# A hybrid decoder layer on one Trainium2 core: attention's steps no longer fall within an output pair's last call of matmuls

## The chip, the core and the metric

The kernel runs on one core of a Trainium2 chip. Five engines matter here: TensorE (PE in the profile), VectorE (DVE), ScalarE (ACT), GpSimd (POOL) and the queue that issues most DMAs (SP). Each engine works through its own instructions in the order in which the program was built, and waits for the others by semaphores. The metric is the device time of one execution in microseconds; the median of three runs of the kernel before is 2708.38 us, the lowest 2703.49 and the highest 2708.49.

## What is computed

One layer of a decoder trunk, for 512 tokens of width 2048, in float32. Cut to what matters:

```python
h    = rmsnorm(x, attn_norm_g)
proj = h @ w_in                       # 2048 -> u, v_sgu, q, k, v_att (1024 each), g_a, g_b (2048 each)
y_a  = u * (tril(w_s) @ rmsnorm(gelu(v_sgu)) + b_s)          # per chunk of 128 tokens
# stick-breaking attention, 8 heads of 128, per block of 128 queries:
z        = q @ k.T * Dh ** -0.5
log_1m   = where(strict, log_sigmoid(-z), 0)
tail     = cumsum(log_1m, reverse=True) - log_1m
w        = where(strict, exp(log_sigmoid(z) + tail), 0)
y_b      = w @ v
merged = sigmoid(g_a) * (y_a @ w_up_a) + sigmoid(g_b) * (y_b @ w_up_b)
x = x + merged @ w_o
x = x + swiglu(rmsnorm(x))            # hidden width 5632
x = x + sigmoid(rmsnorm(x) @ w_ple_gate) * (p @ w_ple)
```

The change concerns the projection by `w_in` and the attention that runs beside it. Everything behind that stage is the same in both kernels.

## The kernel before, in words

**Pairs and calls.** A `Pair` makes 256 columns of a projection for all 512 tokens. In the stage of `w_in` it works by Strassen's seven products (`PRODUCTS`), with a high and a low part of each operand. The sum over the 2048 rows is cut into four calls of `Pair.add`, each with the weights of two blocks of rows. A call has 32 matmuls: products 0 to 4 have four each at L629, each into one of five whole PSUM banks ("ps"), and the last two have six each at L271 to L273, into the halves of a sixth bank. In the pair's **last call** (`stop`, L615), `mix_doubled` (L675 on) adds the finished products on DVE (L688) with copies by ACT (L685) while the call's other products are still being made.

**The order of work in the first stage.** `order` lists what the pairs make: q, k, v of round 0 (two heads each), then four gate blocks, then q, k, v of round 1 and three gates, round 2 and three gates, round 3 and four gates; then the eight blocks of the spatial gating and the last two gates. So a round has six or seven pairs, and its attention runs beside the pairs that follow its k.

**Ticks.** Within each call, `tick()` is called after the fourth product (i = 3) and after the seventh (i = 6) (`TICKS`, L643). A pair has four calls and so eight ticks; the seventh and eighth lie within its last call. A tick takes from the heap `waiting` whatever is due and lets it emit its next instructions. `beside(steps, first)` (L249) puts a generator there: `step` runs it to its next `yield n` and puts itself back n ticks later. What a tick emits is tied to stand behind the matmuls already emitted (`add_manual_dep`, L214); a scheduler then decides how far behind them.

**Attention.** A round's attention (L1013 on) is such a generator. It starts six ticks behind its k and makes one step a tick. For each of 8 blocks (two heads, j from 3 down to 0, (4 - j)*128 query columns) there are stages with these lines:

- stage a: z on PE into a small bank ("small", of which there are two) (L1034), scaled and through Abs, Exp, Ln on ACT (L1036 to L1039)
- stage m: two sums on DVE (L1043, L1045), a mask on POOL (L1047), and a copy and a memset of row 0 on POOL (L1054, L1055)
- stage b: the high part on ACT (L1058); stage c: the low part on DVE (L1062)
- stage d: two matmuls with a triangle of ones on PE (L1068 with the high part, L1069 with the low part, called tri 1 and tri 2 below), a subtraction on DVE (L1073, for j > 0 also L1071), the exponential on ACT (L1074), a mask on POOL (L1075)
- `finish(h)` after the four blocks of a head: the product with v on PE (L1084), a copy on ACT (L1086). Its first matmul reads block j = 0, the last one that was made.

A block i (0 to 7) has its steps b, c, d at ticks 9 + 3i, 10 + 3i and 11 + 3i behind k; `finish(0)` stands with step c of block 4 at tick 22, `finish(1)` at tick 34. q, k and v have their own preparation (`q_prep`, `k_prep`, `v_prep`): transposes on PE (L959), squares on ACT (L966), a power on POOL (L976) and scalings on ACT (L981).

**Weights.** Each call's weights come through one of the landing buffers. SP issues two DMAs for them (L316 and L318, "wholes<-w_in"). When they have landed, POOL issues a third one that adds to what landed (L338, in `landed`). Then ACT rounds them to a high part (L334), DVE makes sums (L350) and low parts (L331), and the buffer is free for SP's next load once DVE has read it. POOL's DMA issues stand in one queue with its masks.

Of the kernel before, what the change touches and what calls it, by code (L numbers as in the profile page):

```python
# [65 lines left out]
def hybrid_layer(  # L66
# [93 lines left out]
    def fits(sizes):  # L160

        before = parts.holes, wholes.holes
        parts.holes, wholes.holes = list(parts.holes), list(wholes.holes)
        try:
            for arena, n, how in sizes + [(wholes, 1024, "low")]:
                arena.take(n, how)
            return True
        except ValueError:
            return False
        finally:  # L170
            parts.holes, wholes.holes = before

    def wide():
        return tmp.tile([P, 1024], F32, tag="out", name=nm("out"))
# [7 lines left out]


    clock = [0]
    waiting = []
    newest = {}
    builds = deque()

    def mark(instruction):
        newest[instruction.ins.engine] = instruction.ins.name  # L190

    def after(n, fn):
        heapq.heappush(waiting, (clock[0] + n, next(names), fn))

    def traced():
        return nc.cur_bb.bb.instructions

    def tick():

        clock[0] += 1  # L200
        last, units = traced()[-1], dict(newest)
        for f in list(builds)[:AHEAD]:
            if not f.there and f.ready() and fits([(wholes, 1024, "old"), (wholes, 1024, "low")]):
                f.fetch()
                break
        if builds and builds[0].ready() and builds[0].arrived() and fits(builds[0].sizes):
            builds.popleft().step()
        while waiting and waiting[0][0] <= clock[0]:
            heapq.heappop(waiting)[2]()
        for i in reversed(traced()):  # L210
            if i is last:
                break
            if i.engine in units:
                tc.add_manual_dep(  # L214
                    i, units[i.engine],
                    mybir.DependencyInfo(mybir.DependencyClass.NoSync,
                                         mybir.DependencyReason.DATA),
                    reason="in its place among the units")
# [27 lines left out]
                self.advance()  # L246
            return self.result

    def beside(steps, first=1):  # L249


        def step():
            n = next(steps, None)
            if n is not None:
                after(n, step)

        after(first, step)
# [11 lines left out]
    def mm3(ps, sh, sl, mh, ml, start, stop, halved=False):  # L269
        for s in (slice(0, 256), slice(256, T)) if halved else (slice(None),):  # L270
            nc.tensor.matmul(ps[:, s], sh, mh[:, s], start=start, stop=False)  # L271
        nc.tensor.matmul(ps, sh, ml, start=False, stop=False)  # L272
        return nc.tensor.matmul(ps, sl, mh, start=False, stop=stop)  # L273
# [109 lines left out]
    def prepare_early():  # L383

        if prepared:
            prepared[0].to(4)
        if len(prepared) > 1 and (slots or prepared[1].step > 1):
            prepared[1].to(3)

    def prepare_late():  # L390

        if len(prepared) > 1 and prepared[1].step > 1:
            prepared[1].to(4)
        for w in list(prepared)[2:]:
            w.to(1)
        ahead(8)
# [175 lines left out]
    class Pair:  # L572
# [21 lines left out]
        def add(self, kind, ws, xs, prepare=True):  # L594
            n = len(ws)
            start = self.left[kind] == self.n[kind]
            self.left[kind] -= n
            stop = self.left[kind] == 0
            if prepare:
                prepare_early()  # L600
            if kind == "P":
                for u, ((wh, wl), (xh, xl)) in enumerate(zip(ws, xs)):
                    for ps, bs in zip(self.ends(), ((2, 3), (0, 1))):
                        for k, b in enumerate(bs):
                            first = start and u + k == 0

                            mark(mm3(ps, wh[:, b], wl[:, b], xh[k], xl[k],
                                     first and not self.both, stop and u == n - 1 and k == 1,
                                     first and self.both and b < 2))
                    if prepare and u == 0:  # L610
                        prepare_late()
                    tick()
                return

            if stop:  # L615
                o = self.home()
                self.o = wide() if o is None else o
                mix = (self.mix_doubled if self.doubled else self.mix)(self.o)
            for i, ((name, h), (w, x)) in enumerate(zip(HALVES, PRODUCTS)):
                for u, ((wh, wl), t) in enumerate(zip(ws, xs)):  # L620
                    first, last = start and u == 0, stop and u == n - 1
                    if i < self.doubled:
                        ps = self.at(i)
                        both = ps, wh[:, w], t[:, x].rearrange("p s c -> p (s c)")
                        low = ps[:, :256], wl[:, w], t[:, x, 0]

                        work = (low, both) if u else (both, low)
                        for k, (out, l, r) in enumerate(work):
                            m = nc.tensor.matmul(out, l, r, start=first and k == 0,  # L629
                                                 stop=last and k == 1)  # L630
                        mark(m)
                    else:


                        ps = self.at(name)[:, 256 * h : 256 * h + 256]
                        ends = not (self.both and name in "yz") and (h == 1 or name == "z")
                        mark(mm3(ps, wh[:, w], wl[:, w], t[:, x, 0], t[:, x, 1],
                                 first and h == 0, last and ends))
                if stop:
                    next(mix)  # L640
                if i == 2:
                    prepare_late()
                if i in TICKS[n]:  # L643
                    tick()

        def mix(self, o):

# [205 lines left out]
    def rms_tile():  # L853
        return tmp.tile([P, 8], F32, tag="rr", name=nm("rr"), bufs=4)
# [87 lines left out]
    def a_tiles():  # L942

        for tag, n in (("l", T), ("w0", T), ("w1", 3 * P), ("w2", 2 * P), ("w3", 2 * P),
                       ("first", 5 * P), ("k", 1024), ("v", 1024), ("zs", 1024)):
            att[tag] = take(n)
        for tag in ("zh", "zl"):
            att[tag] = parts.take(T, "high")

    def a_tile(tag, n=T, start=0):  # L950
        return att[tag].f(start, start + n)
# [50 lines left out]
    def k_prep(o, rk):  # L1002
        for h in range(2):
            yield 2
            token_rms(flip(o[:, h * T : (h + 1) * T]), rk[:, NT * h : NT * (h + 1)])
        nc.scalar.activation(o, o, AF.Copy, scale=gcol[:, g_k : g_k + 1])
# [156 lines left out]
    def block(w, i):  # L1163

        if w == "k":
            return a_tile("k", 1024)
        if w == "s":
            y_a[i] = take(1024)
            return y_a[i].f()
# [56 lines left out]
    for n, ((w, i), pr) in enumerate(zip(order, made())):  # L1226
        if n == 0:
            row1 = norm1.row()
            nc.vector.tensor_scalar(out=eps_cols, in0=norm1.mean, scalar1=EPS, scalar2=None,
                                    op0=ALU.mult)  # L1230
        if n == 0:
            a_tiles()
        o = pr.out(block(w, i) if n < 3 else None)
        if w == "q":
            beside(q_prep(o, i))
        elif w == "k":
            kT, rk = o, rms_tile()
            beside(k_prep(kT, rk))
            beside(attention(i, kT, rk, a_tile("v", 1024)), 6)
        elif w == "v":  # L1240
            beside(v_prep(o, a_tile("v", 1024)))
        elif w == "s":
            scaled(o, row1)
            nc.scalar.activation(o, o, AF.Gelu_apprx_tanh)
            beside(sgu_v(i, o))
        elif w == "u":
            scaled(o, row1)
            nc.scalar.activation(o, o, AF.Gelu_apprx_tanh)
            nc.vector.tensor_tensor(out=y_a[i].f(), in0=o, in1=y_a[i].f(), op=ALU.mult)
            y_done["a", i] = True  # L1250
        else:
            d = tc.dram_tile([P, 1024], F32, name=nm("gsp"))
            nc.sync.dma_start(out=d, in_=o)
            gate_spill[w, i] = d
# [92 lines left out]
    for c, kinds in enumerate(PASSES):  # L1347
        units, first = hs[at : at + len(kinds)], at
# [139 lines left out]
```

## Time and profile before

| what | value |
|---|---|
| median of three runs | 2708.38 us |
| the three runs | 2708.38, 2708.49, 2703.49 us |
| span of the profiled execution, first to last instruction | 2701.9 us |
| PE busy | 2668.1 us, 99% of the span |
| DVE busy | 2147.0 us, 79% |
| ACT busy | 1367.3 us, 51% |
| POOL busy | 459.0 us, 17% |
| mean TensorE clock granted | 0.997 of full |

The profiled execution's span is 6.5 us under the median of the runs; its time from outside is not among the numbers shown. The stage with the attention lies between about 87 us and 640 us of the span. "Busy" on PE is modelled: a matmul's row is longer than the distance to the next one, since they are pipelined, so a stall is somewhat longer than the idle time that the profile gives. "[0.88 <-DVE parts L1062]" at the end of a row of the timeline is the idle time of the engine before it, and what ended it.

### The profile page before, as it was taken

The page shows a single profiled execution, that of the slowest core. Times are in us where ns is not written, and L with a number is a line of the kernel's source. Part 1 is how long each engine was busy: PE and PEld are TensorE (multiplying, and loading weights), DVE is VectorE, ACT ScalarE, POOL GpSimd, SP SyncE. Part 2 cuts the span into 40 slices and gives each one's busy share as a digit, 9 for nine tenths or more (in the row PEclk, how much of TensorE's full clock was granted, in tenths as well). Part 3 has the DMA queues.
Part 4 walks back from the last instruction along what each step waited for, and adds up shares of the span by engine and source line. Part 5 has one row for each costly group of instructions (what it writes and reads, how often), then busy time and mean ns, then how long its engine had stood idle before and what let it go on. Part 6 is the DMA issues. An engine that isn't in the chain of part 4 may idle for free.

```text
span 2701.9 us, 43167 instructions
## 1 busy us (share of the span) xinstructions
PE 2668.1 (99%) x15875; PEld 2354.6 (87%) x15875; DVE 2147.0 (79%) x3621; ACT 1367.3 (51%) x2143; POOL 459.0 (17%) x543
## 2 busy tenths in 40 slices
PE   8999999999999999999999999999999999999999
PEld 6888888989998889988888888888888999988898
DVE  7687878787887566688988888888889667688776
ACT  7656565655554343374444444444445344453543
POOL 0232323232220000001111111111111111110110
PEclk9999999999999999999999999999999999999999
DMA  7677777777776467678888888888887668688784
GB/s 224 156 185 175 181 173 186 170 187 197 177 186 197 140 173 200 173 219 211 212 212 202 200 203 205 201 198 210 195 210 206 181 167 262 184 249 236 218 243 133
DMA packets 303268, 529.40 MB, mean 196 GB/s; under 512 B 25680, under 2 KB 162896, under 8 KB 303056
## 3 DMA queue, kind: packets, MB, share of 16 engines
q1 hardware_dynamic: 242304, 426.22, 49.9%
q0 software_dynamic: 60752, 100.43, 23.8%
q8 instruction: 124, 2.03, 0.3%
q14 instruction: 88, 0.72, 0.1%
HBM read 479.36 MB, written 47.19 MB: 195 GB/s over the span
## 4 chain that ended last, share of the span: by engine, by line
PE 88%; DVE 5%; DMA 2%; ACT 2%; issue 1%; POOL 1%; SPq 0%; DVEq 0%; ACTq 0%; POOLq 0%
PE ps L629 39%; PE ps L272 14%; PE ps L273 14%; PE ps L271 14%; PE small L629 4%; DVE wlo L331 2%; DVE out L688 1%; PE small L1084 1%; PE small L959 1%; ACT whi L334 1%; DMA wholes<-w_in 0%; DMA wholes<-w_first 0%; DVE wholes L350 0%; PE small L1034 0%; DVE parts L267 0%
## 5 line engine op out<-in xcount | busy, mean ns | idle before, releaser
L334 ACT ACTIVATE whi<-wholes 128x512 fp32r<-128x512 f32 (+4 forms) x950 | 857.6, 917 | 838.3 <-DVE wholes L350 261.9
L629 PE MATMUL ps<-parts,whi 128*128 128x512 f32 x3384 | 1134.8, 398 | 0.3 <-DVE p L688 0.3
L331 DVE TENSOR_TENSOR wlo<-wholes,whi 128x512 fp32r<-128x512 f32 (+4 forms) x950 | 962.4, 1046 | 101.0 <-ACT whi L334 100.5
L271 PE MATMUL ps<-parts,whi 128*128 128x256 f32 (+1 forms) x2675 | 855.1, 323 | 15.7 <-ACT parts L266 9.7
L272 PE MATMUL ps<-parts,whi 128*128 128x256 f32 (+1 forms) x2640 | 857.0, 325 | 1.0 <-DVE parts L267 0.8
L273 PE MATMUL ps<-parts,wlo 128*128 128x256 f32 (+1 forms) x2640 | 855.9, 325 | 0.9 <-DVE wlo L331 0.9
L629 PEld LDWEIGHTS ps<-parts,wlo 128*128 128x128 f32 x3384 | 635.8, 188 | 142.6 <-issue 1.0
L629 PE MATMUL ps<-parts,wlo 128*128 128x256 f32 x3384 | 671.1, 279 | 0.0
L271 PEld LDWEIGHTS ps<-parts,whi 128*128 128x128 f32 x2675 | 508.8, 190 | 60.7 <-ACT parts L266 10.8
L629 PEld LDWEIGHTS ps<-parts,whi 128*128 128x128 f32 x3384 | 545.3, 189 | 5.0 <-issue 1.0
L272 PEld LDWEIGHTS ps<-parts,whi 128*128 128x128 f32 x2640 | 502.7, 191 | 47.2 <-DVE parts L267 2.8
L273 PEld LDWEIGHTS ps<-parts,wlo 128*128 128x128 f32 x2640 | 502.7, 191 | 41.2 <-DVE wlo L331 2.8
L350 DVE TENSOR_TENSOR wholes<-wholes 128x256 f32<-128x256 f32 (+1 forms) x794 | 326.8, 412 | 21.8 <-DMA wholes<-w_ffn_out 4.0
L338 POOL DMA_DIRECT2D wholes<-w_ffn_in x172 | 149.7, 871 | 693.0 <-DVE wholes L350 238.8
L688 DVE TENSOR_TENSOR out<-out,ps 128x256 f32<-128x256 f32 x388 | 160.3, 415 | 131.7 <-ACT out L685 131.5
L338 POOL DMA_DIRECT2D wholes<-w_in x132 | 118.0, 895 | 486.1 <-DVE wholes L350 145.7
L655 DVE TENSOR_TENSOR out<-out 128x256 f32<-128x256 f32 x144 | 60.9, 423 | 114.7 <-ACT out L652 112.2
L629 PE MATMUL small<-parts,whi 128*128 128x512 f32 x344 | 136.5, 397 | 0.0
L267 DVE TENSOR_TENSOR parts<-wholes,parts 128x1024 fp32r<-128x1024 f32 (+4 forms) x131 | 123.7, 950 | 14.9 <-ACT parts L266 14.5
L266 ACT ACTIVATE parts<-wholes 128x1024 fp32r<-128x1024 f32 (+4 forms) x131 | 105.8, 834 | 42.0 <-DVE wholes L497 20.0
L338 POOL DMA_DIRECT2D wholes<-w_ffn_out x56 | 56.9, 1020 | 403.4 <-DMA wholes<-w_ffn_out 139.6
L1328 ACT ACTIVATE out<-out 128x512 f32<-128x512 f32 x44 | 27.8, 633 | 157.9 <-DVE out L1327 157.9
(121 smaller groups left out, 1655.0 us busy)
## 6 DMA issues: line engine op xcount, KB each, us to landing
wholes<-w_ffn_in SPq DMA_DIRECT2D x172, 384.0 KB, 5.6
wholes<-w_in SPq DMA_DIRECT2D x132, 384.0 KB, 4.9
wholes<-w_ffn_in SPq DMA_DIRECT2D x172, 256.0 KB, 4.8
wholes<-w_ffn_in POOLq DMA_DIRECT2D x172, 256.0 KB, 5.4
wholes<-w_in SPq DMA_DIRECT2D x132, 256.0 KB, 4.2
wholes<-w_in POOLq DMA_DIRECT2D x132, 256.0 KB, 5.0
wholes<-x SPq DMA_DIRECT2D x33, 512.0 KB, 5.5
wholes<-w_ffn_out SPq DMA_DIRECT2D x31, 512.0 KB, 4.5
```

Source lines behind the costliest of these rows:

```text
L266: return (nc.scalar.activation(hi, src, AF.Copy), nc.vector.tensor_tensor(out=lo, in0=src, in1=hi.bitcast(F32), op=ALU.subtract))
L267: nc.vector.tensor_tensor(out=lo, in0=src, in1=hi.bitcast(F32), op=ALU.subtract))
L271: nc.tensor.matmul(ps[:, s], sh, mh[:, s], start=start, stop=False)
L272: nc.tensor.matmul(ps, sh, ml, start=False, stop=False)
L273: return nc.tensor.matmul(ps, sl, mh, start=False, stop=stop)
L331: in_turn(nc.vector.tensor_tensor(out=self.lo[:, blocks], in0=r, in1=h.bitcast(F32), op=ALU.subtract))
L334: in_turn(nc.scalar.activation(h, r, AF.Copy))
L338: nc.gpsimd.dma_start(out=raw[:, 3:5], in_=self.src[:, 1:3], accum_op=ALU.add)
L350: in_turn(nc.vector.tensor_tensor(out=o, in0=x, in1=y, op=ALU.add))
L629: m = nc.tensor.matmul(out, l, r, start=first and k == 0, stop=last and k == 1)
L655: in_turn(nc.vector.tensor_tensor(out=out, in0=x, in1=y, op=op))
L688: in_turn(nc.vector.tensor_tensor(out=out, in0=x, in1=y, op=op))
```

## The change

Attention's generator is put into the heap with `apart=True`. While a pair's last call of matmuls is being emitted (`mixing[0]`), its step does nothing and puts itself back for the next tick. So the steps that were at the seventh and eighth tick of a pair come with the first tick of the next pair's first call, and all later steps of the round move with them. `q_prep`, `k_prep`, `v_prep` and the steps of the spatial gating stay as they were. No instruction is added or taken away.

```diff
+    mixing = [False]
...
-    def beside(steps, first=1):
+    def beside(steps, first=1, apart=False):
...
         def step():
+            if apart and mixing[0]:
+                after(1, step)
+                return
             n = next(steps, None)
             if n is not None:
                 after(n, step)
...
+            mixing[0] = stop
             if stop:
                 o = self.home()
...
                 if i in TICKS[n]:
                     tick()
+            mixing[0] = False
...
-            beside(attention(i, kT, rk, a_tile("v", 1024)), 6)
+            beside(attention(i, kT, rk, a_tile("v", 1024)), 6, apart=True)
```

## The prediction

> **What bounds the kernel now.** I read the page first, then the stretches of time pair by pair, then the tile "small" (all of attention's banks), then the timeline around each idle time of PE that this tile shows.
>
> ```profile
> PE 2668.1 (99%) x15875; PEld 2354.6 (87%) x15875; DVE 2147.0 (79%) x3621; ACT 1367.3 (51%) x2143; POOL 459.0 (17%) x543
> PE 88%; DVE 5%; DMA 2%; ACT 2%; issue 1%; POOL 1%; SPq 0%; DVEq 0%; ACTq 0%; POOLq 0%
> L629 PE MATMUL ps<-parts,whi 128*128 128x512 f32 x3384 | 1134.8, 398 | 0.3 <-DVE p L688 0.3
> ```
>
> PE is the bound, nearly without a break, so the change is worth what it takes from or adds to PE's waits. The third row answers the question that the change itself raises: does the evacuation in a last call (DVE L688) hold the matmuls up? In 3384 matmuls it did so for 0.3 us. Taking attention's DVE steps out from between these additions has no direct gain to bring. What remains are PE's waits for attention:
>
> ```profile
> core 0: us, PE busy (x) PEld busy (x) DVE busy (x) ACT busy (x) POOL busy (x), PEclk, DMA share, GB/s
> 616.32:636.10 19.78, 19.78 (x130) 17.95 (x129) 15.62 (x27) 8.71 (x13) 4.36 (x5) 1.00 0.88 219
> 334.49:339.43 4.94, 4.94 (x35) 4.50 (x33) 2.94 (x4) 1.80 (x3) 0.86 (x1) 1.00 0.76 157
> 320.31:326.59 6.28, 5.40 (x34) 4.64 (x33) 6.25 (x13) 1.35 (x3) 1.65 (x3) 1.00 0.74 216
> 326.59:334.49 7.90, 7.33 (x42) 5.82 (x41) 5.24 (x8) 3.06 (x5) 1.79 (x2) 1.00 0.93 240
> ...
>   DVE parts L1062: 3.6, 4
>   POOL wholes L1075: 2.2, 4
> ```
>
> A pair with nothing beside it takes 19.78 us, a call 4.94 us. The last two rows (idle time before matmuls of "small", us and times) say that PE waited four times, once a round, for step c of the last block, and four times for the last mask before finish(1). Both lie in the pair of the next round's q (in round 3, a gate): its first call took 6.28 us, its second 7.90 us.
>
> ```profile
> 322.74 0.50 PE L1069 MATMUL small<-parts,tri 128*128 128x512 f32 x1 [0.88 <-DVE parts L1062]
> 327.55 0.70 PE L1084 MATMUL small<-wholes 128*128 128x512 f32 x1 [0.57 <-POOL wholes L1075]
> ...
> 321.34 0.41 DVE L688 TENSOR_TENSOR out<-out 128x256 f32<-128x256 f32 x1
> 322.01 0.68 DVE L1062 TENSOR_TENSOR parts<-wholes,parts 128x512 fp32r<-128x512 f32 x1
> ...
> 325.50 0.90 POOL L338 DMA_DIRECT2D wholes<-w_in  x1 [4.63 <-DVE wholes L350]
> 326.35 1.14 POOL L1075 TENSOR_SCALAR_AFFINE_SELECT wholes<-wholes 128x128 f32<-128x128 f32 x1
> ...
> 292.44 2.42 PE L1084 MATMUL small<-wholes 128*128 128x512 f32 x8
> 294.62 0.36 PE L629 MATMUL ps<-parts,wlo 128*128 128x256 f32 x1
> ```
>
> Step c of block 7 stood in DVE's queue among the last call's additions, so tri 2 came late. Of the first call, 6.28 - 4.94 - 0.23 (one tri pass, 512 columns) = 1.1 us is loss. finish costs PE 294.62 - 292.44 = 2.2 us where it does not wait, so the second call lost 7.90 - 4.94 - 2.2 = 0.7 us. These are the four rounds' prizes: 1.1 and 0.7 us each, 7.2 us together.
>
> **The change part by part.** A pair has eight ticks; ticks 7 and 8 are barred now. The 28 steps from tick 7 to 34 behind k come at ticks 9 to 14, 17 to 22, 25 to 30, 33 to 38 and 41 to 44.
>
> *Blocks in mid-round.* Steps c and d now always fall on ticks 1 and 2, or 4 and 5, of a pair. Both placings exist before (blocks 5 and 6) and cost PE no recorded wait. Stages a and m only come later, and ACT, POOL and DVE have ticks to spare behind them. I take 0; were a tri 2 to wait as block 7's did, it would be 1.1 us.
>
> *Block 7.* Its c comes at the first tick of the next k's pair, behind the additions, and its d at the second. In the built order tri 2 stands nine matmuls into the second call, at 4.94 + 0.2 + 1.6 = 6.7 us of the pair. Block 5 is the model for c:
>
> ```profile
> 298.76:320.31 21.55, 21.55 (x138) 19.02 (x137) 18.99 (x37) 14.08 (x24) 8.37 (x12) 1.00 0.71 184
> 304.25 0.42 DVE L1062 TENSOR_TENSOR parts<-wholes,parts 128x256 fp32r<-128x256 f32 x1
> ...
> 310.48 0.40 ACT L1074 ACTIVATE wholes<-wholes 128x256 f32<-128x256 f32 x1
> 310.95 0.36 POOL L1075 TENSOR_SCALAR_AFFINE_SELECT wholes<-wholes 128x128 f32<-128x128 f32 x1 [0.94 <-ACT wholes L1074]
> ```
>
> It started 304.25 - 298.76 = 5.5 us into its pair; with 0.68 us for 512 columns c ends at 6.2. The wait goes: -1.1 us a round (bounds -1.1 and 0).
>
> *finish(0)* moves from a last call to the third call of its pair, ten matmuls in: 2 x 4.94 + 1.0 (tri and z) + 1.6 = 12.5 us. The mask it needs ended, in block 5's like case, 310.95 + 0.36 - 298.76 = 12.55 us into the pair. So no slack is left, and DVE's next L331 may run beside the mask. L1075 takes between 0.3 and 4.1 us (the row stands further down). I take +0.5 us a round (0 to 1.4).
>
> *finish(1)* moves to tick 4 of the k pair. There it meets q's preparation and POOL's queue. In the built order POOL has there, in rounds 0 to 2: weights DMA (L338), q's power (L976), weights DMA (L338), the last mask (L1075). In the kernel before, the mask stands in the q pair, behind a DMA that had long been ready (the row at 325.50). What the second L338 waits for shows in the k pairs of before, which start at 208.38, 344.38 and 480.34:
>
> ```profile
> 344.38:365.37 20.99, 20.99 (x143) 19.16 (x141) 16.22 (x30) 12.32 (x26) 4.61 (x5) 1.00 0.69 164
> 208.38:229.40 21.02, 21.02 (x142) 19.18 (x141) 16.23 (x30) 12.31 (x26) 4.61 (x5) 1.00 0.66 163
> 480.34:501.33 20.99, 20.99 (x142) 19.16 (x141) 16.23 (x30) 12.31 (x26) 4.61 (x5) 1.00 0.70 176
> 352.47 0.38 SPq L316 DMA_DIRECT2D wholes<-w_in  x1
> 355.53 1.37 POOL L976 TENSOR_TENSOR rr<-ms,expo 128x4 f32<-128x4 f32 x1
> 221.58 0.93 POOL L338 DMA_DIRECT2D wholes<-w_in  x1 [0.53 <-issue]
> 357.53 0.92 POOL L338 DMA_DIRECT2D wholes<-w_in  x1 [0.63 <-DMA wholes<-w_in]
> 492.79 0.94 POOL L338 DMA_DIRECT2D wholes<-w_in  x1 [1.05 <-DMA wholes<-w_in]
> L1075 POOL TENSOR_SCALAR_AFFINE_SELECT wholes<-wholes x32: 282/769/4122, 131.4 to 598.3; 128x128 f32<-128x128 f32 x32
> ...
> 213.49 2.81 PE ps L629 x16
> 216.31 0.44 PE small L959 x4
> 218.89 3.51 PE ps L629 x20
> ```
>
> The second L338 waits until SP's load has landed (issued at 352.47, released at 357.5), and is through 13.4 to 14.1 us into the pair; c of block 7 (0.68 us), now ahead of the L331 that frees the buffer, may delay it by as much. Then the mask, 0.3 us at the least, 0.77 in the middle. PE comes to finish(1) at 2 x 4.94 + 0.46 (tri) + 0.44 (four transposes) + 9 x 3.51/20 = 12.3 us. So PE waits between 1.4 us (13.4 + 0.3 - 12.3) and 3.3 us (14.1 + 0.68 + 0.77 - 12.3); I take 2.5, near the middle, where it was 0.7: +1.8 us in each of three rounds. Behind PE's wait stands every matmul. In round 3 no q follows and the mask stands ahead of the DMA: -0.7 us.
>
> *The clock.* A wait this long has a second price in this trace:
>
> ```profile
> 2049.04 0.47 PE L271 MATMUL ps<-parts,whi 128*128 128x512 f32 x1 [1.81 <-DVE out L688]
> 2386.54 0.50 PE L271 MATMUL ps<-parts,whi 128*128 128x512 f32 x1 [1.74 <-ACT parts L266]
> 1179.36 0.27 PE L897 MATMUL small<-ones,wholes 128*128 128x1 f32 x1 [1.25 <-DVE wholes L887]
> ...
> 2049.73:2053.13 3.40, 3.40 (x10) 2.65 (x9) 3.40 (x6) 1.15 (x2) 0.00 (x0) 0.50 0.64 209
> 2387.65:2391.05 3.40, 3.40 (x12) 2.82 (x12) 0.38 (x2) 0.00 (x0) 0.97 (x2) 0.50 0.74 203
> 1179.36:1182.76 3.40, 3.40 (x19) 2.97 (x20) 1.42 (x3) 3.01 (x6) 1.03 (x1) 1.00 0.91 339
> ```
>
> Behind idle times of 1.74 and 1.81 us the granted clock (the column PEclk) was 0.50 for 3.4 us; behind 1.25 us it stayed 1.00. Half a clock for 3.4 us loses 1.7 us. At 2.5 us of wait I expect this in two or three of the three rounds: 2.5 x 1.7 = 4.2 us. The Trainium skill ("TensorE: Matmul & The Clock Gate", the table under "Why this matters for your kernels") advises no idle gaps over some 3 us between bursts, since one idle window turns the clock down; by that rule alone a wait of 2.5 us would cost no clock, and the sum would come out 4.2 us lower. The rows above disagree, with drops behind 1.74 us. Part 1 of the page has the window free-running, which would make a drop behind a wait between 1.7 and 3.4 us a matter of phase; no run here shows that yet.
>
> *Other queues.* SP's store of y (512 KB) and the spatial gating's small loads move back with finish(1); the store is read only by the up projections. I take 0. The 0.2 us that z waits behind v's second transposes stays.
>
> *Sum*: rounds 0 to 2, 3 x (-1.1 + 0.5 + 1.8) = +3.6; clock +4.2; round 3, -1.1 - 0.7 + 0.5 = -1.3; together +6.5 us on the span of 2701.9, or 2708.4. The median of the runs stands 6.5 us above that span, so 2714.9 us there.
>
> **The rivals.**
> *The wait grows but the clock holds* (in all or nearly all rounds): 3.6 - 1.3, with at most one drop of 1.7, is +2.3 to +4.0; about 2711.5 us. For it: nothing dropped behind 1.25 us, and 1.4 us is my lower end. Against: my middle lies well over 1.81 us. It is also what the skill's page named above would make of it.
> *The mask comes in time*: if SP's load lands 2 us earlier than in those k pairs (landing under 11 us into the pair), POOL is free before PE arrives. Then both waits go and only finish(0)'s half microsecond is paid: 4 x (-1.1 - 0.7 + 0.5) = -5.2; with finish(0) free -7.2. About 2703 us. Three rows at 12.5 to 13.2 us speak against it.
> *The change doesn't do what it says*: the wait for c goes over to another tri 2 or to the transposes, and finish waits 0.7 us as before: 2708.4 us. Block 7's c, which would end only half a microsecond before PE needs it, leaves some room for that.
>
> **How the numbers follow.** Chances: forecast 0.52, clock holds 0.28, mask in time 0.12, no effect 0.08. 0.2% is 5.4 us, about what a measurement here can tell from no change (the three runs lie 5 us apart). The forecast gives slower in nine cases of ten, the second rival in two of ten, the third rarely: slower 0.53. The rest of these and of the fourth is within 0.2%: 0.36. Faster, nearly all from the third: 0.11. The range reaches down to the third rival's 2703, and up by 3.3 us of wait (0.8 more in three rounds), a drop in each of them (0.9 more) and 0.5 us more at each finish(0) (2 in all): 2714.9 + 5.3, some 2720.
>
> **What would show it.** After: tile "small" has no idle time for DVE L1062; L1084 waits for POOL L1075 some 2 us and more in the k pairs, with L338 just ahead of that mask, and not in round 3; PEclk is 0.50 for 3.4 us behind at least two of these; the q pairs come down to about the 21.55 us of the pair at 298.76, and the k pairs grow from 21.0 by the 2.7 us of moved matmuls and by 2.5 to 4.2 us. A k pair under 24.5 us would prove the forecast wrong, as would an L338 that is through before 12 us of it.

## The result, and the profile after

The changed kernel takes 2718.86 us (median of six runs, 2715.12 to 2728.26) against 2707.14 us of the kernel before, timed beside it (six runs, 2699.06 to 2709.64). The ratio is 1.0051, with a 95% interval of 1.0033 to 1.0068. Timed again later it was 2719.36 us, ratio 1.0055 (1.0042 to 1.0069). So it is slower, as forecast, but by 12 to 14 us and not by 6.5.

The profiled execution took 2715.12 us, the fastest of its six, with a span of 2713.4 us, 11.5 us above that of before. All of this lies in the stage with the attention. First, the four rounds of attention in the view of stretches, cut at the starts of output pairs: pairs 1 to 6, 7 to 12, 13 to 18 and 19 to 23, where pair 5, 11, 17 and 23 is a round's next k (or its counterpart in the last round). The answer's last row gives the sum of the four. The kernel before (114.64 to 636.10 us):

```profile
sum 521.46, PE 514.71 PEld 454.39 DVE 418.70 ACT 314.91 POOL 160.59; mean PE 128.68 PEld 113.60 DVE 104.67 ACT 78.73 POOL 40.15
```

The changed kernel, with the columns as in the prediction (the third number from the end is the granted clock):

```profile
112.58:253.09 140.51, 136.15 (x848) 118.98 (x846) 108.87 (x203) 83.58 (x179) 47.17 (x55) 0.99 0.70 175
253.09:392.45 139.36, 135.20 (x851) 118.89 (x849) 108.18 (x201) 82.07 (x174) 43.28 (x55) 1.00 0.70 174
392.45:532.71 140.26, 135.19 (x850) 118.86 (x849) 108.29 (x201) 82.11 (x174) 45.07 (x55) 1.00 0.71 173
532.71:648.09 115.38, 112.70 (x698) 98.42 (x697) 92.56 (x169) 64.18 (x119) 38.28 (x49) 1.00 0.76 187
sum 535.51, PE 519.24 PEld 455.15 DVE 417.89 ACT 311.94 POOL 173.80; mean PE 129.81 PEld 113.79 DVE 104.47 ACT 77.98 POOL 43.45
```

The rounds grew by 535.51 - 521.46 = 14.05 us: 4.3, 3.4, 4.3 and 2.0. Pair 0, ahead of them, was 2.4 us shorter (25.12 for 27.53 us). Below, a round's time is also given without its half-clock stretches, at 1.7 us each: here one, so 533.8 against 521.5, which is +12.3 us.

Lines of the kernel after stand five to seven lower: L1062 is now L1069, L1069 (tri 2) L1076, L1074 L1081, L1075 L1082, L1084 L1091, L331 L336, L334 L339, L338 L343, L688 L695. What PE waited for ahead of matmuls of "small" (idle us, times), changed kernel:

```profile
  POOL wholes L1082: 14.1, 8
```

The row for step c (DVE) is gone, as forecast. In its place all eight finishes wait for the mask, 14.1 us where it was 2.2 us in four. The timeline around one finish(0), one k pair, and the other rounds' finish(1), changed kernel:

```profile
308.89 1.26 ACT L339 ACTIVATE whi<-wholes 128x1280 fp32r<-128x1280 f32 x1
310.05 0.61 ACT L1081 ACTIVATE wholes<-wholes 128x512 f32<-128x512 f32 x1
310.18 2.19 DVE L336 TENSOR_TENSOR wlo<-wholes,whi 128x1280 fp32r<-128x1280 f32 x2 [0.38 <-ACT whi L339]
310.75 1.08 POOL L1082 TENSOR_SCALAR_AFFINE_SELECT wholes<-wholes 128x128 f32<-128x128 f32 x1 [1.58 <-ACT wholes L1081]
311.88 1.12 PE L1091 MATMUL small<-wholes 128*128 128x512 f32 x2 [1.29 <-POOL wholes L1082]
...
353.48 0.38 SPq L321 DMA_DIRECT2D wholes<-w_in  x1
356.16 0.62 ACT L1081 ACTIVATE wholes<-wholes 128x512 f32<-128x512 f32 x1
358.11 0.92 POOL L343 DMA_DIRECT2D wholes<-w_in  x1 [1.58 <-DMA wholes<-w_in]
358.73 0.69 POOL L1082 TENSOR_SCALAR_AFFINE_SELECT wholes<-wholes 128x128 f32<-128x128 f32 x1
359.47 2.42 PE L1091 MATMUL small<-wholes 128*128 128x512 f32 x8 [2.18 <-POOL wholes L1082]
...
219.08 3.95 PE L1091 MATMUL small<-wholes 128*128 128x512 f32 x8 [2.60 <-POOL wholes L1082]
500.19 1.13 PE L1091 MATMUL small<-wholes 128*128 128x512 f32 x2 [3.30 <-POOL wholes L1082]
637.35 1.12 PE L1091 MATMUL small<-wholes 128*128 128x512 f32 x2 [0.84 <-POOL wholes L1082]
```

In the first group, read upwards: PE waited 1.29 us for the mask; the mask ran 1.08 us beside DVE's splitting of weights; it started late because its exponential had stood behind ScalarE's rounding of weights. The other three finish(0) waited 1.25, 1.32 and 1.31 us. In the second group the exponential was done at 356.78, but POOL stood until 358.11 at the DMA issue that waits for SP's load, and the mask came behind it: the queue that the prediction described. In the last round, where no k follows, the wait is 0.84 us.

Pairs and clock, in the view of stretches of the changed kernel: the pair with finish(0) of round 1, the q pair behind it, the k pairs at 344.51, 203.58 and 483.99; then 3.41 us behind two finish(1):

```profile
297.89:323.13 25.24, 23.95 (x147) 20.75 (x145) 18.61 (x36) 13.31 (x26) 7.58 (x10) 1.00 0.75 178
323.13:344.51 21.38, 21.38 (x136) 18.81 (x135) 20.20 (x38) 12.52 (x21) 7.91 (x11) 1.00 0.71 185
344.51:370.77 26.26, 24.08 (x153) 20.86 (x151) 16.41 (x30) 12.94 (x28) 5.85 (x8) 1.00 0.69 171
203.58:231.90 28.32, 25.64 (x152) 21.48 (x151) 17.73 (x33) 13.17 (x28) 6.07 (x8) 0.94 0.64 158
483.99:511.48 27.49, 24.16 (x152) 20.86 (x151) 16.82 (x30) 12.94 (x28) 5.90 (x8) 1.00 0.69 163
218.78:222.19 3.41, 3.11 (x4) 1.51 (x5) 0.12 (x1) 0.00 (x0) 0.86 (x2) 0.50 1.01 243
500.19:503.60 3.41, 3.41 (x15) 2.50 (x16) 0.00 (x0) 0.60 (x1) 0.89 (x1) 1.00 0.86 180
```

The q pair is down to 21.4 us (forecast: about 21.55), the k pairs are up from 21.0 to between 26.3 and 28.3 us. The clock fell behind the wait of 2.60 us, and not behind that of 3.30 us.

### The profile page after: what moved, and what is told of

Read it like the earlier page. It is cut to its first block, busy times and chain, and to the rows that moved or that the text cites. A ratio compares the mean times of both kernels' runs of the same rounds, so it can differ in the third digit from the quotient of the medians.

```text
span 2713.4 us, 43117 instructions
## 1 busy us (share of the span) xinstructions
PE 2671.2 (98%) x15875; PEld 2355.8 (87%) x15875; DVE 2146.0 (79%) x3621; ACT 1363.7 (50%) x2143; POOL 472.8 (17%) x543
## 4 chain that ended last, share of the span: by engine, by line
PE 85%; DVE 6%; DMA 3%; ACT 3%; POOL 2%; issue 2%; SPq 0%; DVEq 0%; POOLq 0%; ACTq 0%
PE ps L635 36%; PE ps L277 14%; PE ps L276 14%; PE ps L278 14%; PE small L635 4%; DVE wlo L336 2%; DVE out L695 2%; DMA wholes<-w_in 1%; ACT whi L339 1%; PE small L1091 1%; POOL wholes L1054 1%; DVE wholes L355 0%; DMA wholes<-x 0%; DMA wholes<-hid 0%; PE small L966 0%
## 5 line engine op out<-in xcount | busy, mean ns | idle before, releaser
L339 ACT ACTIVATE whi<-wholes 128x512 fp32r<-128x512 f32 (+4 forms) x950 | 858.4, 917 | 864.7 <-DVE wholes L355 306.6
L336 DVE TENSOR_TENSOR wlo<-wholes,whi 128x512 fp32r<-128x512 f32 (+4 forms) x950 | 963.4, 1048 | 89.1 <-ACT whi L339 88.7
L343 POOL DMA_DIRECT2D wholes<-w_ffn_in x172 | 149.7, 871 | 693.7 <-DMA wholes<-w_ffn_in 233.7
L695 DVE TENSOR_TENSOR out<-out,ps 128x256 f32<-128x256 f32 x388 | 160.9, 416 | 130.5 <-ACT out L692 130.2
L343 POOL DMA_DIRECT2D wholes<-w_in x132 | 117.5, 892 | 477.3 <-DVE wholes L355 148.6
L343 POOL DMA_DIRECT2D wholes<-w_ffn_out x56 | 56.9, 1018 | 402.5 <-DMA wholes<-w_ffn_out 136.4
```

What stands on the lines that cost most here:

```text
L336: in_turn(nc.vector.tensor_tensor(out=self.lo[:, blocks], in0=r, in1=h.bitcast(F32), op=ALU.subtract))
L339: in_turn(nc.scalar.activation(h, r, AF.Copy))
L343: nc.gpsimd.dma_start(out=raw[:, 3:5], in_=self.src[:, 1:3], accum_op=ALU.add)
L695: in_turn(nc.vector.tensor_tensor(out=out, in0=x, in1=y, op=op))
```

## The experiments

All ratios are to the kernel before on the same chip. "Rounds" is the sum of the four rounds in the profiled execution, "net" the same less 1.7 us for each half-clock stretch inside.

| kernel | median us | ratio, 95% interval | rounds | stretches | net |
|---|---|---|---|---|---|
| before | 2705.5 to 2707.1 | | 521.5 | 0 | 521.5 |
| changed | 2718.86 | 1.0051 (1.0033 to 1.0068) | 535.5 | 1 | 533.8 |
| changed, again (e9) | 2719.36 | 1.0055 (1.0042 to 1.0069) | 535.5 | 1 | 533.8 |
| e1, masks early | 2714.18 | 1.0027 (1.0015 to 1.0040) | 529.0 | 1 | 527.3 |
| e2, before with masks early | 2705.59 | 1.0000 (0.9991 to 1.0010) | 520.6 | 0 | 520.6 |
| e3, a transfer tied behind the mask | 2717.82 | 1.0048 (1.0034 to 1.0062) | 538.2 | 2 | 534.8 |
| e4, the bar on the tail | 2710.09 | 1.0015 (1.0006 to 1.0024) | 525.1 | 1 | 523.4 |
| e5, e1 and two stores | 2707.45 | 1.0008 (0.9999 to 1.0017) | 521.2 | 0 | 521.2 |
| e6, e4 and masks early | 2705.34 | 1.0002 (0.9994 to 1.0011) | 519.1 | 0 | 519.1 |
| e7, changed and two stores | 2721.10 | 1.0050 (1.0036 to 1.0063) | 537.6 | 3 | 532.5 |
| e8, masks early in the first half | 2723.81 | 1.0061 (1.0049 to 1.0074) | 540.8 | 5 | 532.3 |

**e1: the changed kernel without a mask behind the exponential.** The masked elements of w get -200 ahead of the exponential, in stage m, instead of 0 behind it. So POOL stands in no finish's way.

```diff
             nc.gpsimd.affine_select(out=s[:, :P], in_=s[:, :P], pattern=[[1, P]],
                                     compare_op=ALU.is_gt, fill=0.0, base=0,
                                     channel_multiplier=-1)
+            nc.gpsimd.affine_select(out=w[:, :P], in_=w[:, :P], pattern=[[1, P]],
+                                    compare_op=ALU.is_gt, fill=-200.0, base=0,
+                                    channel_multiplier=-1)
...
             nc.scalar.activation(w, w, AF.Exp)
-            nc.gpsimd.affine_select(out=w[:, :P], in_=w[:, :P], pattern=[[1, P]],
-                                    compare_op=ALU.is_gt, fill=0.0, base=0,
-                                    channel_multiplier=-1)
```

> The changed kernel, with the mask of the weights taken out of stage d: POOL masks w in stage m instead (it puts -200 into the masked places, which the exponential turns to 0), some ticks before it is needed. Theory: the 14.1 us that PE waits before finish in the changed kernel are POOL's, because the mask is the last link and stands behind a weights DMA that waits for its landing, or runs beside DVE's splitting of weights. Then PE's idle time before finish falls under 3 us in all, no wait of over 1.5 us is left in this stage, and the time comes to about 2719 - 11 (waits) - 2 (one stretch at half clock) = 2706 us, a ratio of 0.995 to 1.000 of the kernel before. Rival: the chain before the mask (step c, the subtraction, the exponential behind ACT's rounding of weights) is late by itself, and the mask only stands at its end. Then PE waits for the exponential instead, 8 us and more in all, and the time stays above 2713 us.

The waits at the finishes went (0.11 us at the most is left of each), but the time came down to 2714.18 us only. A new wait had come at the start of the pair behind k (368.00), while k was still being evacuated. Timeline of e1:

```profile
359.40 1.41 SPq L1095 DMA_DIRECT2D y<-wholes  x1
...
366.10 0.69 ACT L1005 ACTIVATE wholes<-small,gcol 128x512 f32<-128x512 f32 x1 [3.19 <-DMA y<-wholes]
...
367.10 0.75 DVE L695 TENSOR_TENSOR wholes<-wholes,ps 128x256 f32<-128x256 f32 x2 [7.19 <-ACT wholes L692]
...
371.37 0.50 PE L635 MATMUL ps<-parts,whi 128*128 128x512 f32 x1 [1.02 <-DVE p L695]
```

finish(1) sends y to memory and gives its buffer back; two ticks later, in the same pair, `q_prep` takes 1024 columns for the next round's q and gets the same ones. Its first copy (L1005) waits on ScalarE until the store has landed; behind it in ScalarE's queue stand the copies that evacuate the call (L692), behind these the additions (L695), and behind these a bank that PE needs. In the kernel before, finish(1) stood a pair earlier, and its trace shows no such wait for the store. The prediction took this at 0.

**e2: the kernel before with the same early masks.**

> The same move of the mask into stage m, in the kernel before. Theory: the four waits for the mask (0.57 us each by the profile, 0.7 with the pipeline) go, the four waits of step c of block 7 (0.9 us) stay: -3 us, ratio 0.999. Set beside the first run it gives what barring the last call is worth when POOL is out of the way: by the theory the first run is 2 to 4 us under this one, since the four waits for c (1.1 us each) go. Rival: the moved steps cost by themselves where they fall on q's preparation and on the first call's splitting of weights; then the first run is no faster than this one.

No change: 1.0000. The four waits for the mask at finish(1), 2.2 us, are gone, but the four finish(0), which did not wait in the kernel before, now wait 0.80 to 0.85 us each. PE's waits for finish's matmuls in e2 (idle us, times):

```profile
  ACT wholes L1077: 2.5, 3
  issue: 0.8, 1
```

L1077 is the exponential in this kernel, which stands behind the rounding of weights on ScalarE. The four waits for the last step c are still there (2.4 us for 3.6).

**e3: the next transfer of weights tied behind the mask.** In POOL's queue the DMA issue that follows in the program is held until the round's last mask is in.

```diff
-                    nc.gpsimd.dma_start(out=raw[:, 3:5], in_=self.src[:, 1:3], accum_op=ALU.add)
+                    d = nc.gpsimd.dma_start(out=raw[:, 3:5], in_=self.src[:, 1:3],
+                                            accum_op=ALU.add)
+                    if last_mask:
+                        tc.add_manual_dep(
+                            d.ins, last_mask.pop(),
+                            mybir.DependencyInfo(mybir.DependencyClass.NoSync,
+                                                 mybir.DependencyReason.DATA),
+                            reason="behind the last mask")
...
-            nc.gpsimd.affine_select(out=w[:, :P], in_=w[:, :P], pattern=[[1, P]],
+            m = nc.gpsimd.affine_select(out=w[:, :P], in_=w[:, :P], pattern=[[1, P]],
...
+            if h == 1 and j == 0:
+                last_mask[:] = [m.ins.name]
```

> The changed kernel, with one tie more: the next weights DMA that POOL issues behind a round's last mask in the program may not stand ahead of it in POOL's queue. Only finish(1) is touched. Theory (the DMA in front makes the wait in the k pairs): the three waits of 2.2 to 3.3 us fall to about 0.9 us, what is left being the exponential and a mask that runs beside DVE's splitting (exponential ended at 356.8, PE came at 357.3); finish(0)'s four waits of 1.3 us stay. Time -6 us from the three waits, and one stretch at half clock less: about 2711 us. Rival (the mask is slow itself): the three waits stay over 2 us.

It moved the wrong transfer. Timeline of e3:

```profile
358.10 0.92 POOL L344 DMA_DIRECT2D wholes<-w_in  x1 [0.75 <-DMA wholes<-w_in]
358.71 1.07 POOL L1090 TENSOR_SCALAR_AFFINE_SELECT wholes<-wholes 128x128 f32<-128x128 f32 x1
359.06 1.57 POOL L344 DMA_DIRECT2D wholes<-w_in  x1
```

The issue that waits for a landing (358.10) comes earlier in the program than the mask and stays ahead of it; the tie held the one behind. The run says nothing against the queue, and nothing for it. It had the ScalarE wait for the store of y, too (3.35 us in the same round).

**e4: the bar put on the tail of a round.** The bar holds from step c of the last block on, until the next round's first stage b takes it away again.

```diff
-            if apart and mixing[0]:
+            if apart and mixing[0] and tail[0]:
...
             stage_b(j)
+            tail[0] = i == len(blocks) - 1
             yield 1
```

> One part of the change alone: only the last steps of a round, from step c of block 7 on, are barred from the last call; all steps before run as in the kernel before. finish(0) so stays where it was, c and d of block 7 come at ticks 1 and 2 of the q pair and finish(1) at its tick 4, where POOL has no power to make and no late DMA in front. Theory: the four waits for c (1.1 us) go, finish(1) waits 0.8 us as it does in round 3 of the changed kernel: -4 us against the kernel before, ratio 0.9985, and no stretch at half clock. Rival (the move of the first 24 steps is what costs, or any move of the last does): no faster than before.

PE's waits at the finishes in e4, in sum, and two of them from the timeline:

```profile
  POOL wholes L1083: 6.0, 4
...
198.46 2.08 PE L1092 MATMUL small<-wholes 128*128 128x512 f32 x2 [2.60 <-POOL wholes L1083]
335.33 1.12 PE L1092 MATMUL small<-wholes 128*128 128x512 f32 x2 [1.14 <-POOL wholes L1083]
```

finish(0) waits no more, and finish(1), which stays in the q pair here, waits 2.60 us once and 1.13 to 1.14 us three times. The loss is 4.6 us in the medians and 1.9 us in the net rounds.

The edit did something else than was meant. The flag is still up when the next round starts, so in rounds 1 to 3 the first two steps wait as well, and the whole round comes two ticks later: its first z stands 2.8 us into the round where it stood 2.4 us ahead of it. Only round 0 has the tail alone late, and it lost 1.7 us and a half-clock stretch (139.60 us for 136.18). The other three lost 0.06, 0.02 and 0.15 us with all their steps moved, where the changed kernel lost 3.4, 4.3 and 2.0. So a later place costs little by itself; in rounds 1 to 3 the loss comes with the places that the change gives to the steps in mid-round (finish(0) among them) and to finish(1) in the k pair.

**e5: e1 with the store of y in two halves.**

```diff
-            if h == 1:
-                nc.sync.dma_start(out=y_spill[rnd], in_=qT)
+            nc.sync.dma_start(out=y_spill[rnd][:, h * T : (h + 1) * T],
+                              in_=qT[:, h * T : (h + 1) * T])
+            if h == 1:
                 give(y_b[rnd])
```

> The kernel of e1 (the masks of w made in the block's own stage m, so that no finish waits for POOL), with the store of y cut in two: the first half's 512 columns go out behind finish(0), the second half's behind finish(1). Theory: what is left of the loss in e1 is ScalarE's wait for the store of y of the round before (q_prep writes the same 1024 columns; 3.19 us before its first copy in the profile of e1), which holds up the evacuation of the v pair. Its first copy then needs only the first half's store, which landed long before. The three v pairs of e1 took 22.4, 23.2 and 25.0 us against 21.4 in the kernel before, a sum of 6.4 with one half-clock stretch in it, so the time falls from 2714.2 to about 2708 to 2710, and the TensorE waits for DVE L695 of 1.0 to 1.3 us go. Rival: the k and v pairs are simply too crowded on ScalarE and VectorE with the deferred steps; then the waits stay and the time is about 2714.

2707.45 us, 6.7 us less than e1. Timeline of e5, the same copy and the same additions:

```profile
361.37 0.69 ACT L1005 ACTIVATE wholes<-small,gcol 128x512 f32<-128x512 f32 x1
362.48 0.42 DVE L695 TENSOR_TENSOR wholes<-wholes,ps 128x256 f32<-128x256 f32 x1 [5.14 <-ACT wholes L692]
```

The copy waited for nothing and started 19.1 us into its pair (which starts at 342.26), where it was 22.0 us in e1 (344.06), and the v pair behind it is back at 21.2 us (e1: 23.2). So the store of y is shown to be what was left in e1.

**e6: e4 with early masks.** The rounds 1 to 3 come two ticks later here, too.

> The kernel of e4 (only the steps behind the last block's stage b wait for the next call) with the masks of w made early as in e1. Theory: in e4 the four finish(1) waits for POOL's mask (2.60, 1.14, 1.14, 1.13 us, with a half-clock stretch behind the first) are its whole loss; without them the time is 2710.1 less 6.0, less some 0.2 at each for starting again and 1.7 for the half clock, about 2702 to 2704, and 1 to 3 us below the kernel before. Rival, from e2: where the mask goes, the exponential of the same block, behind a weights' copy on ScalarE, becomes what a finish waits for (0.8 us at three of the four finish(0) there); then about 2706 to 2709, no better than before.

2705.34 us, no different from the kernel before (1.0002, 0.9994 to 1.0011). The net rounds are 2.4 us shorter than before's, but the medians don't show it. The waits in e6 for a step c (idle us, times, ahead of tri 2):

```profile
  DVE parts L1073: 1.6, 3
```

With the mask gone, a step c is what PE waits for, in block 1 of rounds 1 to 3 and no longer in block 7. No kernel here is measurably faster than the one before.

**e7: the changed kernel with two stores, and nothing else.**

> The changed kernel with the store of y in two halves as in e5, and nothing else. ScalarE waited 3.1 us in three rounds for the store in the changed kernel, but TensorE only 0.25 us behind it in one of them. Theory (a small part here, since the late finish already delays everything behind it): 2718 to 2719, within 1 us of the changed kernel, and the rows of ScalarE's wait for y gone. Rival (the store is a main part of the loss here too): 2713 to 2715.

The ratio, 1.0050, is that of the changed kernel; the net rounds are 1.3 us shorter. ScalarE's wait for y is gone from the rows. Between e7 and e5 only the masks differ: 2721.10 against 2707.45 us, 13.7 us, and 11.3 us of net rounds. While the masks wait, the store of y costs little, since everything behind PE's wait is late anyhow; once they don't, it is the next in line.

**e8: masks early in the first half alone.** As e1, with `if h == 0` before the early mask and `if h == 1` before the late one.

> The changed kernel with the masks of w made early for the first half's four blocks alone, so that finish(0) needs no mask behind its exponential and finish(1) is as in the changed kernel. Theory: finish(0)'s price is the mask's: 1.25, 1.29, 1.32 and 1.31 us and some 0.16 us each for starting again, 5.8 us, so about 2713, and no wait above 0.2 us at finish(0). Rival: the exponential itself comes late behind a weights' copy on ScalarE (as at three finishes of e2, 0.85 us): then a wait of 0.5 to 0.9 us stays, and about 2716.

A miss: 2723.81 us, not 2713. The step itself did what the theory said. PE's waits at the finishes in e8 (idle us, times):

```profile
  POOL wholes L1087: 8.6, 4
  ACT wholes L1085: 1.3, 3
```

The four waits at finish(0), 5.2 us in the changed kernel, are now 0.40 to 0.44 us at three, for the exponential, and no more than 0.4 us at the first. But the net rounds fell by 1.5 us only: PE's waits for the evacuation's additions rose from 0.5 to 3.7 us, with 1.71 and 0.51 us in the q pair of round 0. In this profile the clock took the rest: five stretches, 8.5 us, for one. Stretches of e8 behind its waits, in the view of stretches:

```profile
224.10:230.92 6.82, 6.17 (x15) 4.14 (x16) 0.46 (x1) 0.60 (x1) 1.47 (x3) 0.50 0.84 177
190.02:193.43 3.41, 3.41 (x17) 3.31 (x16) 3.38 (x6) 1.90 (x2) 0.88 (x1) 0.51 0.74 219
367.51:370.92 3.41, 3.41 (x11) 2.53 (x10) 0.00 (x0) 0.60 (x1) 0.25 (x1) 0.50 0.83 234
507.44:510.85 3.41, 3.41 (x9) 2.11 (x8) 0.00 (x0) 0.00 (x0) 0.89 (x1) 0.50 0.91 181
```

All three long finish(1) waits (2.68, 2.38 and 2.70 us) have one behind them here, the first a double one; the row at 190.02 follows the wait of 1.71 us. So the price of the masks is not shown to split by finish: early masks in the first half alone did not make the kernel faster.

**e9: the changed kernel once more.**

> The changed kernel itself once more, for the share of the clock. Theory: which of the 2.2 to 3.3 us waits at finish(1) is followed by a half-clock stretch goes by where the wait falls in a window of 3.41 us that runs by itself, so the unchanged code shows another number of them, at other waits than in the first profile (which had one, behind the first): one to three, each 1.7 us. The waits at finish(0) repeat (1.25 to 1.32 us, within 0.05), and the time is 2716 to 2722. Rival: the order of the work sets it, then again one stretch, behind the first finish(1), and about 2715 to 2717.

One stretch again, but behind another wait. Timeline of e9 at the three finish(1), the stretch behind the third, and POOL's DMA issue ahead of each mask:

```profile
217.87 0.70 PE L1091 MATMUL small<-wholes 128*128 128x512 f32 x1 [1.39 <-POOL wholes L1082]
356.46 1.13 PE L1091 MATMUL small<-wholes 128*128 128x512 f32 x2 [1.79 <-POOL wholes L1082]
496.69 0.79 PE L1091 MATMUL small<-wholes 128*128 128x512 f32 x1 [3.49 <-POOL wholes L1082]
...
497.22:500.63 3.41, 3.41 (x9) 2.05 (x7) 0.00 (x0) 0.00 (x0) 0.89 (x1) 0.51 0.86 159
...
216.44 0.93 POOL L343 DMA_DIRECT2D wholes<-w_in  x1 [0.38 <-issue]
354.71 0.92 POOL L343 DMA_DIRECT2D wholes<-w_in  x1
495.38 0.94 POOL L343 DMA_DIRECT2D wholes<-w_in  x1 [2.78 <-DMA wholes<-w_in]
```

The waits at finish(0) repeat to 0.02 us (1.25, 1.30, 1.32, 1.31), those at finish(1) don't (1.39, 1.79 and 3.49 against 2.60, 2.18 and 3.30): they go with the landing of a transfer. In the first two k pairs of e9 the issue ahead of the mask waited for no landing, and PE waited 1.39 and 1.79 us; in the other four, of both profiles, the issue waited 1.58 to 2.78 us for a landing, and PE 2.18 to 3.49 us. So the two profiles show in part what e3 was to show: without the wait for the landing, 1.4 to 1.8 us are left. The net rounds are the same to 0.1 us. The place of a stretch is not set by the code alone.

## Why the prediction was right in its sign and wrong in its size

The sign was right, and the mechanism at finish(1) was right down to the instruction in POOL's queue. The size was wrong: without clock the prediction's terms gave +2.3 us, and the rounds grew by 12.3. Two steps failed. The term finish(0) was sized by block 5's mask of 0.36 us, at +0.5 us a round, and came to 1.45. And the two terms taken at 0, blocks in mid-round and other queues, came to about 4 us together. By its steps:

- **Block 7's wait for step c, -1.1 us a round**: right. Its row is gone (3.6 us of idle time, 4.2 with the 0.16 us a wait that is worked out below), the q pair shown is at 21.4 us.
- **finish(1) in rounds 0 to 2, +1.8 us each**: right in mechanism, close in size. The waits were 2.60, 2.18 and 3.30 us where 2.5 was taken and 1.4 to 3.3 bounded; with before's 0.53 to 0.57 taken off, 6.4 us in the three against 5.4.
- **finish(1) in round 3, -0.7 us**: wrong. The mask does stand ahead of the DMA there, but it ran 1.09 us beside DVE's splitting, and PE waited 0.84 us where it had waited 0.56: +0.3.
- **finish(0), +0.5 us a round, bounds 0 to 1.4**: mis-sized, and one of the two main misses. The waits were 1.25 to 1.32 us, and some 0.16 us more each until the next matmul (the distance of the two matmuls around the wait of 1.286 us is 1.444 us over the usual): 5.8 us in four rounds for the 2.0 taken. The model was block 5, whose mask took 0.36 us; finish(0) meets block 3's, with a 512-column exponential behind ScalarE's 1.26 us rounding of weights, and a mask that takes 1.08 us beside DVE. e8 splits the price: with the mask out of the way 0.42 us of the 1.3 are left, for the exponential.
- **Blocks in mid-round and other queues, 0 and 0**: wrong together by +4.0 us, what is left of 12.3 after the terms above. Of it 1.2 us are in idle rows (tri 2 in three other blocks 0.4; the evacuation's additions 0.6; z 0.2), some 1.3 us by the 0.16 us that rides on each of these eight or so new waits, and 1.5 us I can't assign. The store of y, named in the prediction as read only by the up projections, has a second dependent: the buffer's next writer. In the changed kernel that is worth some 1.3 us (e7); once the masks are repaired, 6 us (e1 to e5).
- **The rivals**: the first one's condition came, but not its time. The clock held in two of three rounds in both profiles, and by the prediction's other terms that would have given 2711.5 us. The other two did not come: the load landed 13.6 us into the k pair (358.11 - 344.51), where "the mask comes in time" needed 11, and the wait for step c went to no other place of its size.
- **The clock, 2.5 stretches, +4.2 us**: not borne out by the profiles of the changed kernel, which show one each in the rounds (+1.7 us). The mean granted clock over the changed kernel's eleven runs is 0.9963, and 0.9977 over the nine runs of the kernel before beside e9 (0.9972 over the 25 beside e1 to e4); the difference of about 0.001 of 2717 us is some 3 us. So the size was about right for the median run and wrong for the profiled ones, which were the fastest of their sets. The reason given for it, that a wait of about 2.5 us is followed by a stretch in most cases, left out where the wait falls (below).

Terms of the two profiles, of before and after: 5.8 + 6.4 + 0.3 - 4.2 + 4.0 + 1.7 = 14.0 us in the rounds (the 4.0 is what was left over, so the sum closes by itself), less 2.4 us in pair 0, which is not the change's: the wait there for ScalarE is 1.6 to 3.6 us, with or without a half-clock stretch, over the kernels run.

What is shown: the masks at the finishes are the bulk (e7 against e5, 13.7 us of time from them alone, all eight together and their clock included), and the store of y is what comes next (e1 against e5); with both repaired the time is that of the kernel before (e5, 1.0008). What is only argued: that finish(1)'s mask would come in time but for the DMA issue ahead of it. The run that should have moved the issue (e3) moved another, and in e9 1.4 to 1.8 us of the wait stayed where the issue waited for no landing.

On the rule that the prediction weighed: the Trainium skill ("TensorE: Matmul & The Clock Gate", Part 1) has the clock decided by a window of 3413 ns that runs by itself. Here the third finish(1) of the same code waited 3.49 us with a half-clock stretch behind it in one profile, and 3.30 us with none in the other, and every stretch shown is 3.41 us or twice that, which agrees. The page's advice against gaps over some 3 us is too lenient here: in e8 a wait of 2.38 us was followed by one.

The traces show the window itself. The four half-clock stretches of the changed kernel's profile start at 24.22, 218.78, 2399.90 and 2546.67 us; the distances are 57, 639 and 43 times 3.4133 us. Windows of this grid, changed kernel: the one ahead of the stretch at 218.78, and the two into which the wait of 3.30 us fell:

```profile
215.37:218.78 3.41, 1.12 (x6) 0.61 (x4) 2.91 (x5) 2.19 (x7) 1.52 (x3) 1.00 0.84 186
495.26:498.67 3.41, 1.63 (x9) 1.04 (x8) 2.47 (x4) 2.67 (x7) 0.87 (x1) 1.00 0.84 185
498.67:502.09 3.42, 1.90 (x6) 1.14 (x7) 0.55 (x2) 0.00 (x0) 1.56 (x3) 1.00 0.96 233
```

PE was busy for 1.12 us of the first (the second number), and the clock fell at its end; the longer wait was cut into two windows with 1.63 and 1.90 us of work, and the clock held. In e8 and e9 the windows ahead of the stretches at a finish(1) had 0.47 to 1.37 us of work. So what counts is how much of a wait falls into one window. The limit lies near half of it, no sharper than that: the kernel before has windows of 1.59 and 1.67 us of work ahead of its stretches at 2049.73 and 2387.65.

## What to carry to other kernels

When a step is moved, ask for each buffer that it frees who takes it next, and for each transfer that it starts who overwrites its source: the store of y looked as if nobody read it soon, and its source's next writer stood in the queue that evacuates the matmuls. Cost a moved step by the largest of its kind at the place where it will stand, with the neighbours it will have there, and not by a smaller block elsewhere. And where several things end within a microsecond of each other, taking one away is worth little (e2, e6), while putting one later costs its full lateness.

## What the runs showed of the hardware

A POOL mask of 128x128 is stretched by what VectorE does beside it. The masks of stage m, grouped, in the stretch from 88 to 650 us; the kernel before:

```profile
L1047 POOL TENSOR_SCALAR_AFFINE_SELECT wholes<-wholes 128x128 f32<-128x128 f32 x32 | 22.4, 700 | 37.4 <-DVE wholes L1045 37.4
```

The changed kernel:

```profile
L1054 POOL TENSOR_SCALAR_AFFINE_SELECT wholes<-wholes 128x128 f32<-128x128 f32 x32 | 48.2, 1508 | 40.8 <-DVE wholes L1052 40.8
```

The same 32 masks went from a mean of 700 ns to 1508 ns by being moved to ticks at which DVE splits weights from two inputs in SBUF: 24 of them ran beside the splitting (L336), with a mean of 1.86 us, where it had been 10; the other eight took 0.46 us. The shortest of the last masks takes 0.29 us. The Trainium skill ("SBUF — State Buffer", "SBUF: two separate sides") has the port pair that VectorE and GpSimd share as an exclusive lock, held for a whole instruction, also by a VectorE operation with two SBUF inputs against a GpSimd operation that reads SBUF. The rows agree with it: at 310.75 the mask started behind the splitting at 310.18, whose first instruction took 1.49 us, to 311.67; the mask ended at 311.83, after 1.08 us, where it needs 0.29 us alone.

The half-clock stretches were the other surprise: their number behind waits of 1.4 to 3.5 us differs between profiles of one kernel, with where the waits fall in the window of 3.41 us. So a single profile can't price a wait of this length, and the mean clock over many runs is the better measure.
